# Hybrid GatedDeltaNet and retention block with a convolutional MLP: the outputs' sum before the state in a block's last chunk, and the last retention head two chunks earlier

## Chip, cores and metric

The kernel runs on one core of a Trainium2 chip. The metric is the device time of one execution in microseconds; less is better. Every operand is float32.

## The reference

One decoder layer over a sequence of 2048 tokens and a width of 1024: a root-mean-square norm, one input projection for two groups of four heads with 128 columns each, an output projection with a residual, a second norm, a gated MLP (d_ff 2816) with a causal convolution of width 3, a residual and a last norm. The first group is a gated delta net (GDN). Its recurrence over chunks is the part that the change touches:

```python
def step(state, inp):
    u_b, w_c, qk_c, qd_c, kd_c, cd_c = inp
    u = u_b - jnp.einsum('bhck,bhkv->bhcv', w_c, state)
    o = jnp.einsum('bhck,bhkv->bhcv', qd_c, state) + jnp.einsum('bhij,bhjv->bhiv', qk_c, u)
    state = state * cd_c[..., None, None] + jnp.einsum('bhck,bhcv->bhkv', kd_c, u)
    return state, o
...
o = _rms_f32(o) * norm_w.astype(jnp.float32) * jax.nn.silu(gt)
```

The second group is retention (fixed decay per head, rotary on q and k), also chunked, with the same norm and gate on its output. Both outputs are concatenated to `mix` and multiplied by `w_out`.

## The kernel before

The sequence is cut into four blocks of 512 tokens, a block into four chunks of 128 tokens. A program is a list of items; the string `ORDER` names them, the digit in front being the block. Items that matter here: `r{p}{c}` is the recurrence of head pair p in chunk c (`gdn_rec`, with the norm's `gdn_fin` behind chunks 1 and 3), `h{n}` and `y{n}` are the two halves of retention head n (`ret_head`, `ret_out`), `g{p}` and `G{p}` gate, transpose and combine the outputs of pair p of both groups for the block's first and second half (`gated`), `W1` to `W7` are seven products that make the output projection (a Strassen form; `ORDER` runs them 1, 2, 6, 7, 5, 3, 4), `N` is the second norm's transpose and store, and `p`, `a`, `c`, `k0`, `q0` and so on are projections and preparation. After the last block follow `mlp_up` (products into `p`, weights `wu`, operands `x`) and `mlp_down`.

`ORDER` is not the order on the engines. The framework has a scheduler that plays the program through on a timeline of its own and orders the instructions of each engine by it. So a move in `ORDER`, or another order of two lines, can move instructions of every engine in places where the source is untouched. Pools set what can run ahead: the bank pool of the recurrences and of `rr` and `ro` has 2 buffers, the weights of the W products (`wv`) 5.

Matrix products in full precision are made of three: a high and a low half of each operand, `hi*hi + hi*lo + lo*hi` (lines L116 to L118, names `wo` for the output projection and `p` for the MLP). The high half of an operand is an ACT copy, the low half a subtraction on DVE: for the W products `wu` by L917 and L918, for the MLP's `x` by L973 and L974.

A recurrence step on the engines: PE `ks` (both heads' k and q with the state, L714); DVE L717; PE `wps` (L724); DVE L727 makes `u`; PE `sps` (L732), four products in one bank, two for the state (`kd`, shown as `kv`) and two for the output (`A`, shown as `AT`); DVE L734 twice updates the two states; DVE L737 adds to the outputs `o`; ACT L740 squares them. Behind chunks 1 and 3 DVE L750, and on POOL the power L752, finish the norm's factor. Then DVE L435 forms `mix`, PE L437 transposes it (`mxt`), ACT L440 copies it out (`co`, `og`), DVE L442 to L445 combine it, and ACT L917 and DVE L918 split it for a W product. W1 takes the GDN heads of a block's first half, W2 the retention heads of the first half, W6 a combination of both of the second half with the first.

A retention head: PE `rr` (L818), DVE L810, transposes `rtr` (L826), `rkk` (L832), then `ro` (L846, L847), an ACT copy (L849), four ACT squares (L852), DVE L856, POOL L857, and L435 as above.

In the last block `ORDER` has, before the change, the recurrences of pair 1, then `3g0 2W4 3p1 3G0 2N`, then retention head 3 (`3h3 3y3`), then `3g1 3G1` and the W products.

Of the kernel before, what the change touches and what calls it, by code (L numbers as in the profile page):

```python
# [11 lines left out]
ALU = mybir.AluOpType  # L12
# [39 lines left out]
P = 128  # L52
S = 2048
D = 1024
# [3 lines left out]
NT = TB // P  # L58
# [160 lines left out]
def mixers(ctx, tc, base, base_used, marks, drp, mm3, gamma, mhalf, n1w, n2w, gcw, gv127, epsr, gnw, n2d, hd,  # L219
           x, xT, w_kq, w_v, w_g, w_rk, w_r0, w_r, w_o, rows, masks, rot):  # L220
    nc = tc.nc
    PE, ACT, DVE, POOL = nc.tensor, nc.scalar, nc.vector, nc.gpsimd
# [9 lines left out]
    def pc(*shape):  # L232
        n = int(np.prod(shape))
        i = next((i for i in range(len(pers)) if used[i] + n <= U1), len(pers))
        if i == len(pers):
            pers.append(cp.tile([P, U1], F32, name=f"pers{i}"))
            used.append(0)
        t = pers[i][:, used[i]:used[i] + n]
        used[i] += n
        return t.rearrange("p (a b) -> p a b", a=shape[0]) if len(shape) == 2 else t  # L240
# [27 lines left out]
    Sst = [pc(P) for h in range(NH)]  # L268
# [49 lines left out]
    def half(owner, key, tag, i):  # L318

        if key not in owner:  # L320
            owner[key] = al(tag, [P, 2, TB])
        return owner[key][:, i]
# [7 lines left out]
    def rbank(nm):  # L330
        return psr.tile([P, 512], F32, tag="rc", name=nm)
# [4 lines left out]
    def small(nm, n=16, bufs=2):  # L336
        if nm not in ring:
            ring[nm] = [pc(bufs, n), 0, bufs]
        e = ring[nm]
        e[1] += 1  # L340
        return e[0][:, e[1] % e[2]]
# [13 lines left out]
    def A_items(b, st):  # L355
# [343 lines left out]
        def gdn_rec(hs, c):  # L699
            def f(_):  # L700
                sl = slice(c * P, (c + 1) * P)
                H = [st["hd", h] for h in hs]
                if c == 0:
                    so = small("so", 8, 3)
                    st["so", hs] = so[:, :4], so[:, 4:]
                    for i, (h, e) in enumerate(zip(hs, H)):
                        e["o"] = half(st, ("op", h // 2), "o", h % 2)
                        e["so"] = [so[:, k:k + 1] for k in (2 * i, 2 * i + 1, 4 + 2 * i, 5 + 2 * i)]
                jj = [c * NH + h for h in hs]
                n = len(hs)  # L710
                ps = rbank("ks")
                for k in range(2):
                    for i, (h, e) in enumerate(zip(hs, H)):
                        PE.matmul(ps[:, (k * n + i) * P:(k * n + i + 1) * P], e["ykq"][:, k, sl], Sst[h],  # L714
                                  start=True, stop=True)
                for i, e in enumerate(H):
                    DVE.scalar_tensor_tensor(e["vp"][:, sl], ps[:, i * P:(i + 1) * P], st["neg"][:, jj[i]:jj[i] + 1],  # L717
                                             e["vp"][:, sl], op0=ALU.mult, op1=ALU.add)
                for i, e in enumerate(H):
                    ACT.activation(e["o"][:, sl], ps[:, (n + i) * P:(n + i + 1) * P], AF.Copy,  # L720
                                   scale=st["eg"][:, jj[i]:jj[i] + 1])
                ps = rbank("wps")
                for i, e in enumerate(H):
                    PE.matmul(ps[:, i * P:(i + 1) * P], e["TT"][:, sl], e["vp"][:, sl], start=True, stop=True)  # L724
                h2 = lambda t: t.rearrange("p (i d) -> p i d", i=n)
                u = small("u", n * P, 2)
                DVE.tensor_tensor(h2(u), h2(ps[:, :n * P]),  # L727
                                  h2(st["brk", hs[0] // 2])[:, :, c:c + 1].to_broadcast([P, n, P]), op=ALU.mult)
                ps = rbank("sps")
                for k, w in enumerate(("kd", "A")):  # L730
                    for i, e in enumerate(H):
                        PE.matmul(ps[:, (k * n + i) * P:(k * n + i + 1) * P], e[w][:, sl], u[:, i * P:(i + 1) * P], start=True, stop=True)  # L732
                for i, h in enumerate(hs):
                    DVE.scalar_tensor_tensor(Sst[h], Sst[h], st["eg"][:, 16 + jj[i]:17 + jj[i]], ps[:, i * P:(i + 1) * P],  # L734
                                             op0=ALU.mult, op1=ALU.add)
                op = st["op", hs[0] // 2][:, :, sl]
                DVE.tensor_tensor(op, h2(ps[:, n * P:]), op, op=ALU.add)  # L737
                for i, e in enumerate(H):
                    jk = small("jk", P, 1)
                    ACT.activation(jk, e["o"][:, sl], AF.Square, accum_out=e["so"][c])  # L740
            return f
# [593 lines left out]
```

## Time and profile before

| | |
|---|---|
| median of 3 runs | 2459.84 us (2457.41 to 2461.82) |
| the profiled execution | 2460.31 us |
| its span | 2458.5 us |
| mean granted TensorE clock | 0.996 |
| instructions | 35801 |
| HBM read, written | 405.32 MB, 199.59 MB |

PE is TensorE's matmuls, PEld its weight loads, DVE VectorE, ACT ScalarE, POOL GpSimd, SP the engine that issues most DMAs. A row of the timeline reads: start in us, duration, engine, line, operation, written and read names, shapes, count; in brackets the idle time of the engine just before and what ended it. The order of the engines in the building of the program has no times; all times come from the trace.

### The profile page before, as it was taken

To read this page: it belongs to the slowest core of one execution; us is meant where nothing else is said; L and a number is where in the kernel's file an instruction comes from. 1 tells how busy PE (TensorE), PEld (TensorE's weight loads), DVE (VectorE), ACT (ScalarE), POOL (GpSimd) and SP (SyncE) were. 2 spreads that over 40 slices of the span, in tenths; PEclk is the share of its full clock that TensorE was granted. 3 is DMA by queue.
4 is the path that set the end of the run, shared out by engine and by line. 5 is a ranking of instruction groups with operands and counts; after the bars stand their busy time and mean duration, and the time that the engine had idled before them with its cause. 6 is when DMAs were issued, how large, how long until landed. Compare 5 with 4: busy or idle time off the path is not lost.

```text
span 2458.5 us, 35801 instructions
## 1 busy us (share of the span) xinstructions
PE 2397.2 (98%) x12476; PEld 2016.0 (82%) x12476; DVE 1596.7 (65%) x3157; ACT 998.8 (41%) x2152; POOL 532.7 (22%) x877
## 2 busy tenths in 40 slices
PE   8998899999999999998999999999999999999998
PEld 7887788788888878887888888888888888888887
DVE  5855777444754563447888988896556577454674
ACT  6644535344442552336454344442122234332341
POOL 1354245621047105240000000000000002421030
PEclk9999999999999999999999999999999999999999
DMA  8856589674765656654998878877667778775773
GB/s 327 277 187 218 214 310 343 223 247 175 268 228 180 211 186 222 224 184 181 349 365 313 303 290 300 290 280 250 233 239 258 270 259 281 243 224 156 220 242 112
DMA packets 287477, 607.29 MB, mean 247 GB/s; under 512 B 41088, under 2 KB 121152, under 8 KB 287296
## 3 DMA queue, kind: packets, MB, share of 16 engines
q1 hardware_dynamic: 270720, 590.70, 68.7%
q10 hardware_dynamic: 16576, 14.30, 1.9%
q8 instruction: 98, 1.61, 0.3%
q14 instruction: 83, 0.68, 0.1%
HBM read 405.32 MB, written 199.59 MB: 246 GB/s over the span
## 4 chain that ended last, share of the span: by engine, by line
PE 84%; POOL 5%; DMA 4%; DVE 3%; issue 2%; ACT 2%; SPq 0%; ACTq 0%; POOLq 0%; DVEq 0%
PE p L116 11%; PE p L118 11%; PE p L117 11%; PE d L118 6%; PE d L116 6%; PE d L117 6%; PE tok L399 4%; PE tok L401 4%; PE tok L400 4%; PE chm L116 3%; PE chm L117 3%; PE chm L118 3%; POOL pers L639 2%; POOL pers L637 2%; PE wo L116 2%; PE wo L117 2%
## 5 line engine op out<-in xcount | busy, mean ns | idle before, releaser
L117 PE MATMUL p<-x,wu 128*128 128x512 f32 x1176 | 457.7, 389 | 0.0
L116 PE MATMUL p<-x,wu 128*128 128x512 f32 x1176 | 452.7, 389 | 0.0
L118 PE MATMUL p<-x,wu 128*128 128x512 f32 x1176 | 450.0, 389 | 0.0
L399 PE MATMUL tok<-wc,n 128*128 128x512 f32 (+2 forms) x768 | 276.5, 365 | 19.5 <-ACT n L387 9.6
L400 PE MATMUL tok<-wc,n 128*128 128x512 f32 (+2 forms) x768 | 276.6, 361 | 1.1 <-DVE wc L296 1.1
L401 PE MATMUL tok<-wc,n 128*128 128x512 f32 (+2 forms) x768 | 275.1, 361 | 0.0
L116 PEld LDWEIGHTS p<-x,wu 128*128 128x128 f32 x1176 | 220.8, 188 | 46.4 <-DVE uc L1053 0.4
L118 PEld LDWEIGHTS p<-x,wu 128*128 128x128 f32 x1176 | 220.8, 188 | 45.8
L117 PEld LDWEIGHTS p<-x,wu 128*128 128x128 f32 x1176 | 220.8, 188 | 45.8
L1095 DVE SCALAR_TENSOR_TENSOR acc<-uc,base,acc 128x1023 f32<-128x1023 f32 (+1 forms) x176 | 221.0, 1280 | 39.2 <-ACT acc L1092 38.9
L1053 DVE TENSOR_TENSOR uc<-p,uc 128x512 f32<-128x512 f32 x224 | 153.6, 689 | 134.8 <-PE p L118 131.6
L186 POOL TENSOR_TENSOR vt<-vr 128x512 f32<-128x512 f32 x44 | 66.0, 1504 | 633.0 <-DMA vr<-in_w_d 465.8
L399 PEld LDWEIGHTS tok<-wc,n 128*128 128x128 f32 x768 | 146.1, 191 | 41.0 <-ACT n L387 9.6
L117 PE MATMUL d<-v,uu 128*128 128x512 f32 x448 | 174.3, 389 | 0.0
L118 PE MATMUL d<-v,uu 128*128 128x512 f32 x448 | 174.3, 389 | 0.0
L116 PE MATMUL d<-v,uu 128*128 128x512 f32 x448 | 174.3, 389 | 0.0
L400 PEld LDWEIGHTS tok<-wc,n 128*128 128x128 f32 x768 | 146.5, 191 | 20.8 <-DVE wc L296 1.5
L401 PEld LDWEIGHTS tok<-wc,n 128*128 128x128 f32 x768 | 145.3, 191 | 19.8
L116 PE MATMUL chm<-n,wc 128*128 128x512 f32 x384 | 151.7, 395 | 0.0
L118 PE MATMUL chm<-n,wc 128*128 128x512 f32 x384 | 151.2, 394 | 0.0
L117 PE MATMUL chm<-n,wc 128*128 128x512 f32 x384 | 150.8, 393 | 0.0
L1092 ACT ACTIVATE acc<-uc,base 128x1024 f32<-128x1024 f32 x88 | 97.2, 1144 | 86.2 <-DVE uc L1053 45.1
(250 smaller groups left out, 4723.3 us busy)
## 6 DMA issues: line engine op xcount, KB each, us to landing
wu<-wu SPq DMA_DIRECT2D x308, 512.0 KB, 5.9
wc<-wd SPq DMA_DIRECT2D x168, 512.0 KB, 5.2
wv<-wo SPq DMA_DIRECT2D x84, 512.0 KB, 5.2
wd<-wc SPq DMA_DIRECT2D x60, 512.0 KB, 4.8
ur<-au SPq DMA_DIRECT2D x56, 512.0 KB, 5.5
wur<-in_w_u SPq DMA_DIRECT2D x44, 512.0 KB, 6.5
au<-st SPq DMA_DIRECT2D x88, 256.0 KB, 4.7
vr<-in_w_d SPq DMA_DIRECT2D x77, 256.0 KB, 5.0
```

The source lines that it names most:

```text
L116: PE.matmul(ps, ah, bh, start=(first and i == 0), stop=False, skip_group_check=chk)
L117: PE.matmul(ps, ah, bl, start=False, stop=False, skip_group_check=chk)
L118: PE.matmul(ps, al, bh, start=False, stop=(i == n - 1), skip_group_check=chk)
L186: POOL.tensor_tensor(tt[:, j], a, b_, op=ALU.subtract)
L399: PE.matmul(ps, ah, wh, start=(k == 0), stop=False)
L400: PE.matmul(ps, ah, wl, start=False, stop=False)
L401: PE.matmul(ps, al_, wh, start=False, stop=(k == KT - 1))
L637: POOL.tensor_tensor(tm[:, :, :n], Nb[:, j:j + 1, j + 1:].to_broadcast([P, 8, n]), X[:, :, j:j + 1].to_broadcast([P, 8, n]), op=ALU.mult)
L639: POOL.tensor_tensor(X[:, :, j + 1:], X[:, :, j + 1:], tm[:, :, :n], op=ALU.add)
L1053: add = lambda o, ps, a: DVE.tensor_tensor(o, ps, a, op=ALU.add)
L1092: ACT.activation(acc, u, AF.Copy, scale=mcw[:, ci, 2:3])
L1095: DVE.scalar_tensor_tensor(acc[:, t:], u[:, :T2 - t], w, acc[:, t:], op0=ALU.mult, op1=ALU.add)
```

## The change

In the last chunk of a block (c = 3; eight of the 32 recurrence steps) the two output products precede the two state products in the bank, and the sum into `o` precedes the two state updates. The other chunks keep their order. In `ORDER` the last block's retention head 3 stands between the recurrences of chunks 1 and 2 of pair 1, where it stood behind `2N`.

```diff
-         "2W3 3a3 3c3 3kq 3y1 3f3 3e3 3p0 3l0 3r00 3r01 3r02 3r03 3h2 3y2 3b1 3l1 3r10 3r11 3r12 3r13 "
-         "3g0 2W4 3p1 3G0 2N 3h3 3y3 3g1 3G1 3W1 3W2 3W6 3W7 3W5 3W3 3W4 3N")
+         "2W3 3a3 3c3 3kq 3y1 3f3 3e3 3p0 3l0 3r00 3r01 3r02 3r03 3h2 3y2 3b1 3l1 3r10 3r11 3h3 3y3 3r12 "
+         "3r13 3g0 2W4 3p1 3G0 2N 3g1 3G1 3W1 3W2 3W6 3W7 3W5 3W3 3W4 3N")
...
-                for k, w in enumerate(("kd", "A")):
+
+                last = c == NT - 1
+                ik = n if last else 0
+                for k, w in enumerate(("A", "kd") if last else ("kd", "A")):
                     for i, e in enumerate(H):
                         PE.matmul(ps[:, (k * n + i) * P:(k * n + i + 1) * P], e[w][:, sl], u[:, i * P:(i + 1) * P], start=True, stop=True)
+                op = st["op", hs[0] // 2][:, :, sl]
+                if last:
+                    DVE.tensor_tensor(op, h2(ps[:, :n * P]), op, op=ALU.add)
                 for i, h in enumerate(hs):
-                    DVE.scalar_tensor_tensor(Sst[h], Sst[h], st["eg"][:, 16 + jj[i]:17 + jj[i]], ps[:, i * P:(i + 1) * P],
-                                             op0=ALU.mult, op1=ALU.add)
-                op = st["op", hs[0] // 2][:, :, sl]
-                DVE.tensor_tensor(op, h2(ps[:, n * P:]), op, op=ALU.add)
+                    DVE.scalar_tensor_tensor(Sst[h], Sst[h], st["eg"][:, 16 + jj[i]:17 + jj[i]],
+                                             ps[:, (ik + i) * P:(ik + i + 1) * P], op0=ALU.mult, op1=ALU.add)
+                if not last:
+                    DVE.tensor_tensor(op, h2(ps[:, n * P:]), op, op=ALU.add)
```

The diff adds six lines in `gdn_rec`, so what stands below it moves by six: the sum is L738 (last chunk) or L743, the state update L740, the squares L746, `gdn_fin` L756 and L758, the operand's halves L923 and L924, the x halves L979 and L980, the W adds L896 (were L890). The products stand in L735.

Where the engines' orders differ, three places. First PE at the end of the last block, before the change (the last recurrence's `sps`, retention head 3, the transposes, W2):

```order
L118 MATMUL wo<-wv,wu_11737 128x512
L732 MATMUL sps<-pers_1350,kv 128x128 x2
L732 MATMUL sps<-pers_1350,AT 128x128 x2
L818 MATMUL rr<-rv,rk 128x128 x4
L846 MATMUL ro<-rv,Ar 128x128
L847 MATMUL ro<-pers_125,ykq 128x128
...
L847 MATMUL ro<-pers_662,ykq 128x128
L437 MATMUL mxt<-base,mix 128x128 x10
L116 MATMUL wo<-wv,wu_11765 128x512
L117 MATMUL wo<-wv,wu_11765 128x512
```

And after it, from the end of W1 (wu_11737) over W2 (wu_11765, wu_11782) to the start of W6 (wu_11807):

```order
L118 MATMUL wo<-wv,wu_11737 128x512
L437 MATMUL mxt<-base,mix 128x128 x2
L724 MATMUL wps<-kv,AT 128x128 x2
L735 MATMUL sps<-pers_1350,AT 128x128 x2
L735 MATMUL sps<-pers_1350,kv 128x128 x2
L116 MATMUL wo<-wv,wu_11765 128x512
L117 MATMUL wo<-wv,wu_11765 128x512
...
L118 MATMUL wo<-wv,wu_11782 128x512
L437 MATMUL mxt<-base,mix 128x128 x8
L116 MATMUL wo<-wv,wu_11807 128x512
```

`rr` and `ro` of head 3 stand before r12 now, and W2's 24 products stand between the last `sps` and the last eight transposes.

Second DVE at the same place, before (from the state updates of the last recurrence on):

```order
L734 SCALAR_TENSOR_TENSOR pers_125<-pers_125,pers_230,sps 128x128 x2
L737 TENSOR_TENSOR o<-sps,o 128x2x128
L810 SCALAR_TENSOR_TENSOR pers_662<-pers_125,rr 128x128
L810 SCALAR_TENSOR_TENSOR pers_662<-pers_662,rr 128x128 x2
L750 SCALAR_TENSOR_TENSOR pers_662<-pers_662 128x4
L890 TENSOR_TENSOR Cw<-wo,wx 128x512
L810 SCALAR_TENSOR_TENSOR pers_125<-pers_662,rr 128x128
L435 SCALAR_TENSOR_TENSOR mix<-o,pers_662,mix 128x128 x4
L974 TENSOR_TENSOR x_2_12241<-xr,x_2_12241 128x512
L856 SCALAR_TENSOR_TENSOR pers_662<-pers_662 128x4
L435 SCALAR_TENSOR_TENSOR mix<-o,pers_662,mix 128x128 x4
```

And after (from the last recurrence's `u` on):

```order
L727 TENSOR_TENSOR pers_1350<-wps,pers_230 128x256
L924 TENSOR_TENSOR wu_11765<-co,wu_11765 128x512
L924 TENSOR_TENSOR wu_11782<-co,wu_11782 128x512
L738 TENSOR_TENSOR o<-sps,o 128x2x128
L740 SCALAR_TENSOR_TENSOR pers_125<-pers_125,pers_230,sps 128x128 x2
...
L435 SCALAR_TENSOR_TENSOR mix<-o,pers_662,mix 128x128 x4
L980 TENSOR_TENSOR x_2_12241<-xr,x_2_12241 128x512
L980 TENSOR_TENSOR x_2_12244<-xr,x_2_12244 128x512
L896 TENSOR_TENSOR Cw<-wo,Cw 128x512 x2
L442 TENSOR_TENSOR co<-og,co 128x256
L444 TENSOR_TENSOR co<-co,og 128x256
```

Behind the last row come L980, L443, L980, L442, L444, L445, L443 and L445, and then the low half of W6's operand. W2's two low halves (L924) stand before the sum. On ACT two x splits (L979) stand between the third and the fourth of the last four copies L440, and the high half of W6's operand follows the fourth. On SP the loads of W6's weights now stand ahead of the first two stores of the MLP's split weights.

Third PE at the start of block 1's recurrences, before (transposition products `ttps`, then the first `ks`, then projection products `tok`):

```order
L675 MATMUL ttps<-AT,pers_118 32x32 x2
L714 MATMUL ks<-pers_125,ykq 128x128 x4
L400 MATMUL tok<-wc,n_2580 128x512
L401 MATMUL tok<-wc,n_2580 128x512
L399 MATMUL tok<-wc,n_2583 128x512
```

And after:

```order
L675 MATMUL ttps<-AT,pers_118 32x32 x2
L401 MATMUL tok<-wc,n_2599 128x512
L399 MATMUL tok<-wc,n_2599 128x512
L400 MATMUL tok<-wc,n_2599 128x512
L401 MATMUL tok<-wc,n_2599 128x512
L714 MATMUL ks<-pers_125,ykq 128x128 x4
```

Four projection products stand ahead of `ks`.

## The prediction

> **What bounds the kernel now.** I read the page's busy times first, then the granted clock by stretch, then TensorE's (PE's) waits and the timelines of the engines around the longest of them.
>
> ```profile
> PE 2397.2 (98%) x12476; PEld 2016.0 (82%) x12476; DVE 1596.7 (65%) x3157; ACT 998.8 (41%) x2152; POOL 532.7 (22%) x877
> ```
>
> PE is busy for 2397.2 of 2458.5 us. The change takes no matmul away, so it can only move the time in two terms: PE's idle time, 61 us in all, and matmuls run at a lower clock. In the stretches below the columns are start:end and length, then busy time of PE, PEld, DVE, ACT and POOL, granted clock, DMA share and GB/s.
>
> ```profile
> 0.00:216.06 216.06, 199.36 (x1138) 170.46 (x1138) 134.07 (x335) 108.44 (x278) 89.87 (x183) 1.00 0.71 254
> 216.06:222.88 6.82, 4.56 (x11) 3.60 (x12) 2.16 (x4) 4.45 (x11) 1.63 (x7) 0.50 0.14 33
> 222.88:1147.90 925.02, 894.11 (x5599) 767.98 (x5597) 522.78 (x1501) 405.90 (x1142) 313.60 (x568) 1.00 0.65 226
> 1147.90:1158.14 10.24, 6.86 (x21) 5.53 (x22) 8.62 (x21) 6.43 (x17) 1.01 (x1) 0.50 0.72 275
> 1160.00:1185.00 25.00, 25.00 (x112) 20.71 (x111) 25.00 (x43) 13.82 (x25) 0.00 (x0) 1.00 0.99 376
> ```
>
> The clock is full except in two stretches. Each starts inside a long PE wait, which stands in brackets behind the row that ended it:
>
> ```profile
> 218.32 0.80 PE L399 MATMUL tok<-wc,n 128*128 128x512 f32 x1 [5.43 <-ACT mix L412]
> ...
> 479.00 1.16 PE L714 MATMUL ks<-pers,ykq 128*128 128x128 f32 x8 [1.81 <-DVE pers L810]
> ```
>
> The first wait began at 218.32 - 5.43 = 212.89, and the clock halved 3.17 us later; it came back 4.56 us after the first long matmul. A wait of 1.81 us did not halve it. The second stretch is the place of the change, the end of the last block:
>
> ```profile
> 1141.18 0.39 PE L118 MATMUL wo<-wv,wu 128*128 128x512 f32 x1
> 1141.40 0.60 PE L732 MATMUL sps<-pers,kv 128*128 128x128 f32 x4
> 1141.85 0.61 PE L732 MATMUL sps<-pers,AT 128*128 128x128 f32 x4
> 1142.29 1.06 PE L818 MATMUL rr<-rv,rk 128*128 128x128 f32 x8
> ...
> 1144.75 0.39 PE L847 MATMUL ro<-pers,ykq 128*128 128x128 f32 x2
> 1150.18 2.37 PE L437 MATMUL mxt<-base,mix 128*128 128x128 f32 x10 [5.05 <-DVE mix L435]
> 1153.64 0.79 PE L116 MATMUL wo<-wv,wu 128*128 128x512 f32 x1 [1.09 <-ACT wu L917]
> ...
> 1162.92 0.39 PE L116 MATMUL wo<-wv,wu 128*128 128x512 f32 x1
> ```
>
> W1's last product stands at 1141.18, so one 512-column step takes 0.22 to 0.23 us; then come the last recurrence's products (sps) and retention head 3 (rr, ro). PE waits 5.05 us, transposes, waits 1.09 us and starts W2. The 1162.92 row is W6's first. What PE waits for:
>
> ```profile
> 1142.49 0.61 DVE L734 SCALAR_TENSOR_TENSOR pers<-pers,pers,sps 128x128 f32<-128x128 f32 x2 [1.84 <-PE sps L732]
> 1143.02 0.42 DVE L737 TENSOR_TENSOR o<-sps,o 128x256 f32<-128x256 f32 x1
> ...
> 1145.68 1.14 DVE L435 SCALAR_TENSOR_TENSOR mix<-o,pers,mix 128x128 f32<-128x128 f32 x4
> 1146.74 0.68 DVE L974 TENSOR_TENSOR x<-xr,x 128x512 fp32r<-128x512 f32 x1
> 1148.40 0.16 DVE L856 SCALAR_TENSOR_TENSOR pers<-pers 128x4 f32<-128x4 f32 x1 [0.98 <-ACT pers L852]
> 1149.69 1.14 DVE L435 SCALAR_TENSOR_TENSOR mix<-o,pers,mix 128x128 f32<-128x128 f32 x4 [1.12 <-POOL pers L857]
> 1150.74 1.35 DVE L974 TENSOR_TENSOR x<-xr,x 128x512 fp32r<-128x512 f32 x2
> 1152.01 0.42 DVE L444 TENSOR_TENSOR co<-co,og 128x256 f32<-128x256 f32 x1
> 1152.34 0.42 DVE L442 TENSOR_TENSOR co<-og,co 128x256 f32<-128x256 f32 x1
> ```
> ```profile
> 1146.06 0.58 ACT L849 ACTIVATE o<-ro 128x512 f32<-128x512 f32 x1
> ...
> 1152.94 1.17 ACT L917 ACTIVATE wu<-co 128x512 fp32r<-128x512 f32 x2
> ```
>
> The recurrence's own mix was issued at 1145.68 and is not what PE lacked. The wait ends with retention head 3's: ro done, its copy on ACT at 1146.06, four squares, L856 at 1148.40, the power on POOL, its mix at 1149.69.
>
> **The change, part by part.**
>
> *Products and sum first (eight last chunks).* In the built program PE signals the products to DVE only once all four are issued, so the new L738 starts no sooner for the products' order. What is left is its place ahead of two state updates: 1143.02 - 1142.49 = 0.53 us per last chunk. In blocks 0 to 2 no PE wait of this trace ends on that sum, so I count 0 there; what hides it is PE's other queued work, and without that it would be worth at most 8 x 0.53 = 4.2 us. In block 3, two lower halves of W2's operand (L924) now stand ahead of L738 on DVE and eat the gain: by my estimate the sum comes 1.5 us after the first of these products, against 1143.02 - 1141.40 = 1.62 now. The state updates come 0.42 us later; nothing in the block reads that state again.
>
> *Retention head 3 moved: until W1 ends.* rr and ro take 1142.29 to 1144.97, 2.68 us of PE, now ahead of W1's end. The head issues no DMA; on ACT's queue it passes block 2's norm stores, whose readers are the x loads, but these stores go out with the nps transposes, ahead of W1 in both orders. The last wps pair goes behind it (0.45 us, as the pair of sps rows at 1141.40 and 1141.85). The waits inside block 3's recurrences:
>
> ```profile
> PE sps L732 <- DVE pers L727: 2.2, 4, 0.6
> PE wps L724 <- DVE kv L717: 2.0, 4, 0.6
> PE wo L116 <- DMA wv<-wo: 1.1, 1, 1.1
> ```
>
> Eight waits make 4.2 us, 0.52 each. Now the wps of r02, r03, r12 and r13 and the sps of r02, r03, r11 and r12 wait. In PE's new order the wps of r12 (six transposes), of r13 (W1) and the sps of r03 (rkk and transposes) have work in front; the sps of r13 loses W1, and the ks of r03 follows r02's sps directly: seven bare steps, six before W1's end, 6 x 0.52 = 3.1. W1 would end at 1141.40 + 2.68 - 0.45 - (4.2 - 3.1) = 1142.5; I call that M.
>
> *From there to W6.* PE's row has two transposes, wps, sps, W2's 24 products, eight transposes, then W6.
>
> ```profile
> 1107.50 0.68 PE L724 MATMUL wps<-kv,AT 128*128 128x128 f32 x4 [0.54 <-DVE kv L717]
> 1108.70 0.49 PE L732 MATMUL sps<-pers,kv 128*128 128x128 f32 x2 [0.52 <-DVE pers L727]
> ```
> ```profile
> 878.22 0.66 PE L437 MATMUL mxt<-base,mix 128*128 128x128 f32 x4 [0.78 <-DVE mix L435]
> 880.43 0.50 PE L116 MATMUL wo<-wv,wu 128*128 128x512 f32 x1 [1.55 <-ACT wu L917]
> ```
>
> Two transposes 0.22, wps to sps 1.20, sps 0.89 (1141.40 to 1142.29), 24 x 0.227 = 5.45: W2 ends at M + 7.75. The recurrence's mixes are issued at M + 0.22 + 1.20 + 1.5 + (1145.68 - 1143.02) = M + 5.6 and done before that, so PE doesn't wait for them: the 5.05 us wait goes. Eight transposes of 0.11 take it to M + 8.6 = 1151.1.
>
> What is late next is W6's operand, og + co4 - co1 of both heads. Between the transposes and it DVE has, in its new order, two adds for W2 (0.62 each, waiting for W2's last products at M + 7.95), then seven combinations up to the one needed (0.33 each, 1152.01 to 1152.34) with two x lower halves between them (0.62 each): M + 7.95 + 1.24 + 2.3 + 1.24 = M + 12.8; ACT makes the upper half, and PE starts 0.7 us after it (1152.94 to 1153.64). ACT has two x splits ahead of its last og copy too, which adds some 0.2. W6 starts at M + 13.7 = 1156.2, after a new wait of 5.1 us.
>
> Now W6 starts at 1162.92, with seven of the MLP's products (p) done before it that come after it in the new order: 7 x 0.227 = 1.59, so the like point is 1161.3. Gain 1161.3 - 1156.2 = 5.1 us. But a wait of 5.1 us is one that halved the clock twice; the clock came back 4.56 us after long matmuls began in one case and 1158.14 - 1153.64 = 4.50 in the other, and at half speed this costs 4.5 / 2 = 2.25. (What the drop costs now lies in the 1161.3.) Net -2.85 us. Bounds: if only the copies stand between transposes and W6, as at 880.43 (2.21 for four, 2.65 for eight), the wait is 1.8 and the clock stays: 1161.3 - (1142.5 + 7.75 + 2.65) = 8.4 gained; if one load of x that ACT splits there is late by 2 us, the gain is 0.9.
>
> [...]
>
> *Elsewhere.* The scheduler reorders the fill in blocks 1 and 2 as well. At the 479.00 wait four products of 0.227 now stand ahead of ks: -0.9. Other steps lose or gain a filler, each worth 0.5 either way; I take 0 with -2 to +3 for them. DVE is full and DMA at 0.99 in 1160 to 1185, yet PE has no wait there; I count 0.
>
> Sum: -2.85 - 0.9 = -3.75. The profiled execution took 2460.31 us for its span of 2458.5, 0.47 above the median of the runs (2459.84); from the median it gives 2456.1, from the profile 2456.6. Forecast 2456.5.
>
> **The rivals.**
>
> *The stall closes or the clock holds.* With a wait of 5.1 us and no drop, 2460.3 - 5.1 - 0.9 = 2454.3; with the short wait 2460.3 - 8.4 - 0.9 = 2451.0. For it: a gap of 1.55 us before a W at 880.43, and waits under 2 us left the clock alone. Against: DVE's row in between, and both long waits halved the clock.
>
> *The change does nothing that counts.* The sum isn't sooner, and what PE gains at the tail is given back in 1160 to 1185, where DVE has 25.00 of 25.00 and can't go faster: 2460, from the point where W6's start brings forward nothing that DVE hadn't begun earlier. Against: W2's halves and one mix now lie before that stretch, about 2 x 0.62 + 1.06 = 2.3 us of DVE work.
>
> *Slower: loads for the W products.* W2 to W6 now follow each other with fewer p products between, and DMA is at 0.99. One wait for such a load is in the trace, 1.1 us. It decides when the new waits pass the gain of 3.75; eight of 1.1 give 2460.3 - 3.75 + 8.8 = 2465.4. Against: only five W products come after W2, and SP now issues W6's loads earlier.
>
> **How the numbers follow.** 0.2%, 4.9 us, is what a measurement of this kernel can tell from no change. Forecast as worked out, 2453.5 to 2459: 0.40. Clock holds, 2452.5 to 2456: 0.20. Stall closes, 2449 to 2452.5: 0.12. Below 2454.9 lie 0.08 of the forecast's 0.40, 0.16 of the 0.20 and all of the 0.12. Given back, 2459 to 2462: 0.14. Slower, 2462 and up: 0.14, 0.02 of it below 2464.7. Faster 0.36, same 0.32 + 0.04 + 0.14 + 0.02 = 0.52, slower 0.12. The range 2449.5 to 2463.5 leaves out the worst loads and a gain over both bounds; the likeliest case's own is 2453.5 to 2459.
>
> **What would show it.** Right: no mxt row with a wait for L435 over 1 us in the tail; W2 directly behind sps; one wait of 4 to 6 us before W6's first wo, ended by ACT's wu (L923), with the clock at 0.50 behind it; L738 some 1.5 us after sps. Wrong: a wait before W6 under 3 us (the DVE count was too long), a clock that holds, waits for DMA wv in W2 to W3, or new PE waits over 1 us in blocks 1 and 2.

## The result and the profile after

The changed kernel took 2473.71 us (median of 3 runs, 2473.09 to 2475.02) against 2459.84 before: slower by 13.9 us, a ratio of 1.0056 with a 95% interval of 1.0043 to 1.0070. The forecast was 2456.5 with a range that ended at 2463.5. Its profiled execution has a span of 2471.9 us. First the busy times of the changed kernel's page:

```profile
PE 2407.1 (97%) x12476; PEld 2021.9 (82%) x12476; DVE 1593.0 (64%) x3157; ACT 1001.9 (41%) x2154; POOL 529.8 (21%) x877
```

The instructions are the same 12476 on PE, but they kept it busy for 9.9 us more, and it was idle for 64.8 us in place of 61.4. The same work took longer: the mean granted clock was 0.992 in place of 0.996. These are all the changed kernel's stretches at half clock between the start and the last stores (columns as in the prediction; the 0.50 is the granted clock):

```profile
152.08:155.49 3.41, 3.41 (x10) 2.67 (x9) 2.12 (x4) 3.22 (x16) 2.40 (x2) 0.50 0.70 237
213.52:220.35 6.83, 4.64 (x11) 3.68 (x12) 2.24 (x4) 4.53 (x11) 1.56 (x7) 0.50 0.15 33
309.09:315.92 6.83, 6.30 (x15) 4.47 (x15) 5.63 (x12) 5.45 (x25) 0.85 (x1) 0.50 0.81 302
466.10:469.52 3.42, 3.42 (x10) 2.67 (x9) 0.59 (x1) 0.00 (x0) 3.03 (x6) 0.50 0.36 72
633.36:636.77 3.41, 3.41 (x9) 2.59 (x9) 3.41 (x10) 3.36 (x5) 0.00 (x0) 0.50 0.15 37
875.70:882.53 6.83, 5.87 (x26) 5.28 (x26) 2.05 (x8) 2.23 (x10) 0.00 (x0) 0.50 0.24 65
892.77:896.18 3.41, 3.41 (x9) 2.65 (x8) 0.82 (x4) 0.00 (x0) 0.00 (x0) 0.50 0.00 0
1169.25:1172.66 3.41, 2.85 (x7) 2.28 (x8) 3.17 (x6) 3.10 (x6) 0.00 (x0) 0.50 1.03 413
```

Eight stretches where before had two. A 512-column step took 0.43 us in them (467.09 to 467.52) and 0.23 outside (465.72 to 465.95), so half of the PE column's sum, 33.3 / 2 = 16.7 us, is about what they cost; before it was (4.56 + 6.86) / 2 = 5.7. So in this pair of executions 10.9 us are clock and 3.4 us idle time, 14.3 for a span 13.4 longer. The rest lies in the first microseconds, which the prediction had read as full clock. There the steps from product to product were 0.22 us long, and 0.12 us only from 14.67 us on in before, where the profile's record of the clock begins (the columns write 1.00 for the time ahead of it):

```profile
13.70 0.42 PE L399 MATMUL tok<-wc,n 128*128 128x264 f32 x1
13.92 0.42 PE L400 MATMUL tok<-wc,n 128*128 128x264 f32 x1
...
14.87 0.28 PE L399 MATMUL tok<-wc,n 128*128 128x264 f32 x1
14.99 0.28 PE L400 MATMUL tok<-wc,n 128*128 128x264 f32 x1
```

In the changed kernel the short steps began at 12.13 already. PE was busy at the long step for 5.1 us before and for 2.9 us after, and half of the difference, 1.1 us, comes back.

One can also ask at which time each kernel had done the same work on PE (its busy time, counted at half where the clock was half, the start included). So counted, the changed kernel was 2.0 us ahead of before at 300 us, 3.6 behind at 330, 7.4 behind at 700, 13.9 behind from 905 to 1100, 10.5 behind at 1180, when W6 is under way, and 12.9 behind at the end. The tail that the prediction was about gained; blocks 1 and 2 lost. The stretch from 300 to 920 us, before and then after:

```profile
300.00:920.00 620.00, 604.08 (x3652) 516.91 (x3651) 358.45 (x1001) 272.32 (x747) 223.87 (x389) 1.00 0.69 240
```
```profile
300.00:920.00 620.00, 599.43 (x3583) 511.75 (x3582) 346.85 (x976) 268.49 (x740) 218.66 (x388) 0.98 0.67 232
```

PE was idle there for 20.6 us in place of 15.9, and the five half-clock stretches of the changed kernel in it cost 22.4 / 2 = 11.2 us. So most of this loss is the clock, and less of it the waiting itself.

The waits that the changed kernel has there, on PE's timeline:

```profile
303.98 1.25 PE L437 MATMUL mxt<-base,mix 128*128 128x128 f32 x10
308.03 1.09 PE L555 MATMUL kqtr<-base,ykq 128*128 128x128 f32 x8 [2.80 <-ACT co L440]
...
465.38 0.50 PE L399 MATMUL tok<-wc,n 128*128 128x512 f32 x1 [2.82 <-DMA wc<-wd]
...
632.03 0.50 PE L116 MATMUL wo<-wv,wu 128*128 128x512 f32 x1 [2.38 <-ACT wu L923]
...
873.31 0.71 PE L735 MATMUL sps<-pers,kv 128*128 128x128 f32 x4 [1.11 <-DVE pers L727]
...
891.27 0.50 PE L116 MATMUL wo<-wv,wu 128*128 128x512 f32 x1 [2.02 <-ACT wu L923]
```

Of these lines only L735 stands in the diff, and the row shown is not one of a last chunk: there kv comes first, as before. At 303.98 all ten transposes stand together, and the first of the products with ykq wait for a bank, which the copies of the transposes' results set free. Before, eight transposes ran there, and then 13 projection products until 307.86 which covered the copies (PE's timeline of the kernel before):

```profile
304.02 1.03 PE L437 MATMUL mxt<-base,mix 128*128 128x128 f32 x8
304.81 0.48 PE L118 MATMUL chm<-n,wc 128*128 128x512 f32 x1
...
307.62 0.40 PE L118 MATMUL chm<-n,wc 128*128 128x512 f32 x1
307.86 0.38 PE L437 MATMUL mxt<-base,mix 128*128 128x128 f32 x2
```

ACT at the place of the 2.80 us wait, in the changed kernel:

```profile
307.08 0.63 ACT L533 ACTIVATE ykq<-ca 128x512 f32<-128x512 f32 x1 [4.35 <-DVE ca L351]
307.61 0.36 ACT L440 ACTIVATE co<-mxt 128x256 f32<-128x256 f32 x1
```

The copy PE waits for (L440) stands behind a silu that waits for DVE for 4.35 us. At 632 it is ACT again: in the changed order a table load of 1.28 us and a decay matrix that waits 1.30 us for its DMA come ahead of the chain that ends in W's operand.

### The profile page after: what moved, and what is told of

Its sections match the earlier page's. It is cut to its first block, busy times and chain, and to the rows that moved or that the text cites. A ratio compares the mean times of both kernels' runs of the same rounds, so it can differ in the third digit from the quotient of the medians.

```text
span 2471.9 us, 35791 instructions
## 1 busy us (share of the span) xinstructions
PE 2407.1 (97%) x12476; PEld 2021.9 (82%) x12476; DVE 1593.0 (64%) x3157; ACT 1001.9 (41%) x2154; POOL 529.8 (21%) x877
## 4 chain that ended last, share of the span: by engine, by line
PE 85%; POOL 5%; DMA 3%; DVE 3%; issue 2%; ACT 1%; SPq 0%; ACTq 0%; POOLq 0%; DVEq 0%
PE p L116 11%; PE p L117 11%; PE p L118 11%; PE d L118 5%; PE d L116 5%; PE d L117 5%; PE tok L399 5%; PE tok L401 5%; PE tok L400 5%; PE chm L116 3%; PE chm L118 3%; PE chm L117 3%; POOL pers L639 2%; POOL pers L637 2%; PE wo L116 2%; PE wo L117 2%
## 5 line engine op out<-in xcount | busy, mean ns | idle before, releaser
L1101 DVE SCALAR_TENSOR_TENSOR acc<-uc,base,acc 128x1022 f32<-128x1022 f32 (+1 forms) x176 | 220.8, 1279 | 39.9 <-ACT acc L1098 39.7
L347 DVE SCALAR_TENSOR_TENSOR ca<-ca,base 128x511 f32<-128x511 f32 x144 | 112.6, 782 | 32.2 <-ACT ca L344 31.4
```

The source lines that it names most:

```text
L347: DVE.scalar_tensor_tensor(acc[:, s:], ps[:, :TB - s], w, acc[:, s:], op0=ALU.mult, op1=ALU.add)
L1101: DVE.scalar_tensor_tensor(acc[:, t:], u[:, :T2 - t], w, acc[:, t:], op0=ALU.mult, op1=ALU.add)
```

## The experiments

Theory A: the scheduler, given the sum ahead of the state updates, wrote blocks 1 and 2 in another order, and the waits of that order, with the half clock behind them, are the loss. Theory B: the moved retention head loses the time. Theory C: the sum's new place is dear by itself. In every comparison the kernel before was measured on the same chip together with the variant.

**The moved head alone.** `ORDER` of the change with the recurrence of before.

> Only the move of retention head 3 in the list of items; the recurrence is that of before. TensorE's order of blocks 0 to 2 is then the one before, word for word; only the last block's end differs. Theory A (the loss lies in the fill that the scheduler put elsewhere in blocks 1 and 2 once block 0's last chunk was changed, and in the half-clock windows that the new waits bring; the tail itself gained some 2.6 us up to W6 and gave some 2 back behind it): 2457 to 2461 us, no half clock between 223 and 1140 us, one wait of 4 to 5 us before W6. Theory B (the moved head loses the time, by crowding the last recurrences or the loads behind them): 2468 us or more.

Measured 2460.32 us against 2459.92, ratio 1.0002 (0.9993 to 1.0011): no difference. TensorE's order differs from before only from the last block's recurrences on. B falls. The tail, in stretches of this run:

```profile
1140.00:1158.00 18.00, 14.52 (x78) 11.98 (x76) 13.78 (x35) 8.32 (x24) 1.30 (x2) 1.00 0.79 284
1158.00:1164.83 6.83, 5.04 (x12) 3.98 (x13) 6.56 (x14) 3.95 (x8) 0.00 (x0) 0.50 0.92 366
1164.83:1200.00 35.17, 34.25 (x148) 27.23 (x146) 33.25 (x56) 17.36 (x32) 0.00 (x0) 1.00 0.95 365
```

The wait before W6 is 4.75 us as in the changed kernel, and the half clock follows it. By equal work this run had gained 2.0 us at 1180 and 1.7 us at the end, against its place at 1100 us. One part of the expectation was not met: a window at 881.5 us ran at half clock that hadn't in before's, 1.7 us, though PE's order there is that of before.

**The recurrence alone.** The new recurrence in all blocks, `ORDER` of before.

> Only the recurrence's new order in all eight last chunks; the list of items is that of before. Theory A: the waits at about 308, 448, 465, 632, 766 and 870 to 901 us come back with their half-clock windows, the last block lies some 12.5 us later than before, the 5 us wait before the last transposes stays: 2470 to 2474 us. Theory B: 2458 to 2461 us. Theory C (the state updates behind the sum delay the next block's first recurrence by 0.42 us and the sum itself is dear) would give at most 3 x 0.42 = 1.3 us over before: 2461 us.

Measured 2470.77 us, ratio 1.0045 (1.0032 to 1.0058): most of the loss, without the head. In its profile the half clock came back at 465, 871 and 888 us, but not at 309 and 633, where the waits were 1.82 and 1.11 us here.

**The recurrence in the last block only, with the head.**

```diff
-                last = c == NT - 1
+                last = c == NT - 1 and b == NB - 1
```

> The moved head, and the recurrence's new order in block 3's two last chunks only. Blocks 0 to 2 are ordered as before on TensorE. Theory A: within 2 us of the run with the moved head alone, 2456 to 2461 us; the sum's earlier place is worth 0.5 us at most, since two lower halves stand ahead of it. Theory B: 2468 us or more. If the sum first were itself what costs, this run would be slower than the one with the moved head alone by over 2 us.

Measured 2460.32 us, ratio 1.0002 (0.9993 to 1.0011): the sum first costs nothing where the following blocks aren't rewritten.

**The recurrence in block 0 only, with the head** (`b == 0` in that line).

> The moved head, and the recurrence's new order in block 0's two last chunks only. TensorE's order then departs from before in block 1, and in block 2 in its own way. Theory A: block 1's part of the loss (about 5 us by 700 us of the span) stays, block 2's 6 us are open: 2461 to 2470 us. Theory C: no more than 0.5 us over the run with the head alone.

Measured 2474.25 us, ratio 1.0060 (1.0047 to 1.0073): above what I had expected. Two of the eight steps bring all of it, in block 2 too, although blocks 1 and 2 keep the recurrence of before.

**The products alone.** Output products first in all eight last chunks, the sum behind the state as before.

> The output products ahead of the state's in all eight last chunks, the sum where it was, the list of items that of before. Every engine's order is then that of before but for these eight swaps on TensorE. If the products' order matters by itself (the sum could start after two products), up to 8 x 0.45 us either way. Theory A: it can't, since the products are signalled together and the rest of the order stands: 2458 to 2462 us, no new half clock.

Measured 2455.92 us against 2458.25, ratio 0.9993 (0.9984 to 1.0002): no difference that can be told; the median lies below the range expected. The scheduler leaves nearly all else where it was. Its profiled execution did have two half-clock windows that before's hadn't, at 338.2 and 877.5 us, so "no new half clock" was not met: the waits in front of them, 2.13 and 1.55 us, stand in before too, 2.07 and 1.55, with no half clock behind them.

**One sum, pair 1.** From before, one DVE instruction ahead of two others in one of 32 steps.

```diff
+                first = c == NT - 1 and b == 0 and hs[0] == 2
+                if first:
+                    DVE.tensor_tensor(op, h2(ps[:, n * P:]), op, op=ALU.add)
...
+                if not first:
                     DVE.tensor_tensor(op, h2(ps[:, n * P:]), op, op=ALU.add)
```

> One instruction is moved in the source: in block 0's last chunk of head pair 1 the sum stands ahead of the two state updates; products and list of items are those of before. The scheduler then writes blocks 1 and 2 in another order. Theory A: nearly the whole loss comes back, 2468 to 2475 us, none of it before 300 us of the span although the moved instruction runs near 282 us. Theory C (the sum's place is dear by itself): 2460.5 us at most, since one step of eight is changed.

Measured 2476.18 us, ratio 1.0075 (1.0063 to 1.0088): the whole loss, and 1.2 us above the range expected. In its profile the moved sum runs at 278.39; by equal work the kernel is 2.4 us ahead of before at 300, and 4.1 behind at 700 and 10.3 at 905. ACT and PE at one of its new waits:

```profile
626.20 1.28 ACT L509 ACT_TABLE_LOAD   x1
627.49 0.63 ACT L509 ACTIVATE D<-D 128x512 f32<-128x512 f32 x1
628.14 1.28 ACT L533 ACT_TABLE_LOAD   x1
629.43 0.63 ACT L533 ACTIVATE ykq<-ca 128x512 f32<-128x512 f32 x1
630.08 1.28 ACT L509 ACT_TABLE_LOAD   x1
```
```profile
630.12 1.11 PE L555 MATMUL kqtr<-base,ykq 128*128 128x128 f32 x4 [3.37 <-ACT ykq L533]
```

Here a silu (L533) stands between two exponentials (L509), and a table load of 1.28 us stands ahead of each of the three. There are 23 such loads in this run and in the changed kernel, 21 before. PE waits 3.37 us for the silu's result.

**One sum, pair 0.** The same edit with `hs[0] == 0`. Here the orders of the two kernels agree on every engine but for this one swap on DVE.

> The twin of the run with one moved sum: the same edit in the same chunk of block 0, for head pair 0 instead of pair 1. Here the scheduler leaves every other instruction of every engine where it was; DVE's order differs by that one swap. Theory A (the reordering costs, not the sum): 2457 to 2461 us, no half clock that before may not have. Theory C (a sum ahead of the state updates is dear): some 18 us more like its twin, or at least 2 us.

Measured 2459.88 us against 2459.12, ratio 1.0001 (0.9993 to 1.0010). The twin edit costs 18 us (2476.18 against 2458.25) where the scheduler answers it and nothing where it doesn't. C falls, A stands. The profile of this run has half-clock windows at 152, 340 and 879 us that before's hadn't, though the orders are the same: what the clock took differed by execution, 11.3 us here and 5.7 in before's profile.

**The sum in block 1 only.**

> Only block 1's two last chunks have the sum first; the rest is before. TensorE's order is that of before up to block 2's start and differs in blocks 2 and 3's tail. Theory A: block 2's part of the loss alone, 4 to 8 us: 2464 to 2468 us, with half-clock windows between 600 and 900 us and none before 600 us. Theory C: 2459 to 2461 us.

Measured 2465.10 us (2461.82 to 2470.93) against 2458.25, ratio 1.0033 (1.0021 to 1.0045): a half of the loss, with block 2 and the tail rewritten and block 1 as before. The profiled execution was its shortest, 2461.82 us, with only one half-clock window between 600 and 900 us, at 867.6; the part of the expectation that names several was not met in it. So this loss rests on the times alone, and no profile shows where it lies.

**Work in the wait.** The moved head, and eight products that nobody reads ahead of W6 in the last block:

```diff
+                if i == 6 and b == NB - 1:
+                    pd = bank("wo")
+                    for k in range(NFILL):
+                        PE.matmul(pd[:, :TB // 2], ident, sts[b]["co"][4][:, 3], start=True, stop=True)
```

> The moved head alone, and eight extra products of 128x256 float32 on TensorE ahead of W6 in the last block, whose results nobody reads, placed behind the last transposes; some 3.5 us of work in the wait of 4.75 us. If the clock halves by TensorE's idle time in a window of 3.41 us, it stays full there: 2.5 us less than with the head alone, 2457.8 us, and no half clock between 1140 and 1200 us. If it halves by something else (the number of loads, the activity of other engines), the half clock stays: 2460 us. If the extra products delay W6, slower than 2461 us.

Measured 2457.12 us against 2458.25, ratio 0.9996 (0.9987 to 1.0005). Its tail on PE, where L915 holds the eight products as 16 instructions, and the whole stretch from 1140 to 1200:

```profile
1149.02 1.03 PE L438 MATMUL mxt<-base,mix 128*128 128x128 f32 x8
1150.62 3.72 PE L915 MATMUL wo<-co,base 128*128 128x256 f32 x16 [0.56 <-ACT co L441]
1154.81 0.50 PE L117 MATMUL wo<-wv,wu 128*128 128x512 f32 x1 [0.47 <-ACT wu L922]
```
```profile
1140.00:1200.00 60.00, 57.60 (x260) 46.42 (x259) 56.53 (x102) 30.67 (x59) 1.01 (x1) 1.00 0.94 353
```

The wait is split into 0.56 and 0.47, W6 starts no later for it, and the half clock is gone. Only TensorE was given more to do, so the half clock there came from its idle time, not from the other engines' activity: in the 60 us DVE was busy for 56.53 and ACT for 30.67, with the head alone for 53.58 and 29.64. (The products load weights as well, so this run alone doesn't part idle time from missing loads.) By equal work the 2.5 us show in the profile; in the times (against 1.0002 for the head alone) the two intervals overlap.

**The version the runs point to.** The products' order, the head, the sum where it was, and three more unread products before block 2's W1.

> What the runs point to: the products' order of the change, the moved head, the sum where it was, eight extra products in the wait before block 3's W6 and three in the wait before block 2's W1 (results unread). TensorE's order in blocks 0 to 2 is that of before but for six swaps of products and these three. Theory A with the clock halved by idle time in a 3.41 us window: no half clock between 860 and 900 us nor between 1140 and 1200; 1.7 us less than the run with eight extra products where that one halved, 2 to 5 us below before: 2453 to 2457 us. If extra work before W1 is as dear as the wait it fills, no better than 2457.5 us.

Measured 2457.26 us against 2459.12, ratio 0.9995 (0.9986 to 1.0004): not told from before, and 0.3 us above the range expected. The clock behaved as expected; the stretch from 223 to 2450 us has it at 1.00:

```profile
223.00:2450.00 2227.00, 2195.13 (x11347) 1842.66 (x11345) 1455.94 (x2816) 884.70 (x1861) 443.39 (x687) 1.00 0.71 248
```

Its median is 16 us below that of the changed kernel, taken in another measurement, but no version here beats before beyond the measurement.

PE's idle time and half the busy time at half clock (the start left out), summed for each profiled execution, sort the runs: before 67.1 us; head alone 67.6; head and last block 68.5; products 64.0; one sum in pair 0 68.9; and 81.5 for the changed kernel, 80.1 for the recurrence alone, 81.7 for block 0 only and for one sum in pair 1. The shortest execution of the sum in block 1 has 67.6. Work in the wait and the last version have 58.7 and 58.0, but their unread products, some 3.7 and 5.3 us, count as busy.

## Why the prediction was wrong, point by point

*What failed.* The step "Elsewhere" of the sum. I had seen that the scheduler reorders the fill in blocks 1 and 2, priced the one place where I knew a wait (-0.9) and took 0 with -2 to +3 for the rest, "each worth 0.5 either way". By equal work it came to some 16 us, from 2.0 ahead at 300 to 13.9 behind at 905. Two things made the bound false. The price of 0.5 was that of a bare recurrence step; the reordered engines were also ACT and the DMA queue, and PE waited 2.80 us for a copy behind a waiting silu and 2.82 for a load; with one moved sum in pair 1 it waited 3.37 behind two table loads. Waits for such loads (`wc`) were not longer in sum, though: before had four, 3.7 us together. The larger part is the term that I had put at nothing: I let the clock fall only behind the tail's wait, because a wait of 1.81 us at 479 had left it alone. The new waits of 2.0 to 2.8 us halved it, at 1.7 to 3.2 us a time, and at 875 two short waits together did so for 2.9 us. The prediction's own sign of being wrong, new waits over 1 us in blocks 1 and 2, had named the place. The wait behind the -0.9 did go: none stands before that ks in the changed kernel.

*The slower rival.* It named loads for the W products at the tail and eight waits of 1.1. The changed kernel waited once for such a load, 0.3 us, and no run for more than 1.9 us in all. That the sign was right was luck, for the cause wasn't in it.

*Sum first.* That the products' order gains nothing was right (0.9993 with 1 inside the interval), and that the sum gains nothing at the tail too: L738 ran 1.63 us after the first sps (1.5 forecast), against 1.62 before, behind two lower halves as counted. But the sum's place in the earlier blocks, counted at 0 because no wait ended on it, is what the scheduler answered with another order.

*The tail.* Read from W1's end in the changed kernel, 1156.20:

```profile
1156.20 0.39 PE L437 MATMUL mxt<-base,mix 128*128 128x128 f32 x2
1156.42 0.61 PE L724 MATMUL wps<-kv,AT 128*128 128x128 f32 x4
1157.55 0.71 PE L735 MATMUL sps<-pers,AT 128*128 128x128 f32 x4 [0.52 <-DVE pers L727]
...
1164.02 1.03 PE L437 MATMUL mxt<-base,mix 128*128 128x128 f32 x8
1169.81 0.79 PE L116 MATMUL wo<-wv,wu 128*128 128x512 f32 x1 [4.75 <-ACT wu L923]
```
```profile
1157.97 1.29 DVE L924 TENSOR_TENSOR wu<-co,wu 128x512 fp32r<-128x512 f32 x2 [0.47 <-ACT wu L923]
1159.18 0.42 DVE L738 TENSOR_TENSOR o<-sps,o 128x256 f32<-128x256 f32 x1
...
1161.90 1.14 DVE L435 SCALAR_TENSOR_TENSOR mix<-o,pers,mix 128x128 f32<-128x128 f32 x4 [1.12 <-POOL pers L758]
...
1168.67 0.42 DVE L443 TENSOR_TENSOR co<-co 128x256 f32<-128x256 f32 x1
```

W2 ends 7.8 us after W1 (7.75 forecast), the mixes start at 5.7 (5.6), W6 at 13.6 (13.7) after a wait of 4.75 (5.1), and the 5.05 us wait of before is gone. The half clock followed, for one window of 3.41 us here (1.4 us lost) and two in the run with the head alone (2.5). So the tail's mechanism was right: by equal work the changed kernel had gained 3.4 us between 1100 and 1180 (2.85 forecast). What of it was left is not told by the times: 0.9993 to 1.0011 for the head alone. The profiles give -1.7 by the end for the head alone and -1.0 for the changed kernel. What lies behind W6's start, counted at 0, took some back: a new wait of 1.85 us for an x half at 1207 is part of it.

*The clock holds.* The chance of 0.20 for a wait of 5.1 us with no drop was too high. Only waits under 2 us spoke for it, and behind the clock's first rise no row shows a wait near 5 us that left the clock full: it halved at the waits of 4.98 us (ended at 215.71) and 4.75 (1169.81) in the changed kernel and of 4.75 with the head alone, as at 5.43 and 5.05 in before. At 872.29 us 1.70 us of idle time in 3.41 us sufficed, as the last section shows.

*What stays open.* How the 14 us split into waits and clock differs by execution: the run with one sum in pair 0 lost 11.3 us to the clock and had 57.6 us idle, before 5.7 and 61.4, at spans 0.4 us apart. In the four profiled executions that show the loss it was 14.9 to 16.7 us of clock and 64.8 to 66.8 idle. With one profile for each run, how far either varies for one order isn't known. Which single displaced instruction starts the chain in block 1 wasn't tried.

## What to carry to other kernels

Where a scheduler orders the engines by a timeline of its own, the price of an edit is the price of the orders it writes, and those may change hundreds of us behind the edit. Compare the orders of all engines first: a change that leaves them alone costs its own work, and one that rewrites two stages is a new kernel there, to be priced by a range of the size of that stage's waits and of the half clock behind them (here some 16 us) or held back to a stage with nothing behind it. And two waits of about 1 us close together can cost more than their sum: at 875 us 1.8 us of waiting (1.11 and 0.68) cost 2.9 us of clock on top.

## What the runs showed of the hardware

The half clock came in steps of 3.41 us. In the profiles of before and of the changed kernel the ten stretches at 0.50 ahead of the last stores were 3.41, 6.83 or 10.24 us long, and each began a whole number of steps of 3.413 us behind the clock's first rise, at 14.67 us in before and 12.13 in the changed kernel; so the steps' place against the span's start differed, 1.02 us in the one and 1.89 in the other. The five stretches of the run with one sum in pair 0, at 152.14, 216.99, 339.87, 879.18 and 1148.84 us, stand whole numbers of such steps apart too.

Laid over PE's idle time in these two traces (1413 steps at full clock and 16 at half, from the first rise on), the ten steps at full clock with a half-clock one behind them had 1.70 to 3.41 us idle, and those with full clock behind them 1.70 at most (475.47 in before). That is about half of a step, and it was not always one wait: in the changed kernel the step from 872.29 had its 1.70 us in pieces of 1.02 and 0.68. The length of a wait alone did not tell: waits of 2.02 to 2.82 us were followed by half clock in the changed kernel, waits of 2.07 us (339.66) and 2.35 (151.98) were not in before. The latter, in the first block (kk, L585), put 1.58 us into one step and 0.77 into the next; the same wait of 2.35 us in the changed kernel put its idle time into a step that had 1.98 us, and the clock halved. So it did behind the like row of the run with one sum in pair 0:

```profile
152.15 0.79 PE L585 MATMUL kk<-ykq 128*128 128x256 f32 x1 [2.22 <-DVE pers L814]
```
```profile
152.14:155.56 3.42, 3.41 (x8) 2.76 (x9) 3.38 (x6) 3.28 (x13) 2.20 (x2) 0.50 1.00 388
```

The way back: of the 16 half-clock steps the nine with no idle time were all followed by full clock; of the seven with 0.53 to 2.29 us idle, six were followed by another half-clock step and one, with 0.56, by full clock.
